# One product of 512 columns for both parts of x in the feature-major projections of a two-layer decoder kernel

## The chip, the cores and the metric

The kernel runs on one core of a Trainium2 chip. The metric is the time of one execution on the device in microseconds, as a median of runs. Within the core TensorE multiplies matrices into accumulators in PSUM, VectorE and ScalarE do elementwise work, GpSimd does a little, and SyncE issues the loads and stores. The profile calls them PE, DVE, ACT, POOL and SP; PEld is TensorE's loading of weights.

## The reference

Two layers run over 256 tokens of 2048 features in float32. Each layer normalises its input, projects it to eight branches of 1024 features (the second layer has 16 columns more), lets two mixers work on the branches, gates their results, projects back and adds. The projections are nearly all of the arithmetic:

```python
def even_layer(h, w_in, w_out, ...):
    proj = jnp.einsum('bld,de->ble', h, w_in).astype(f32)
    hq, hf, hi, hz, dq, dk, dv, dz = jnp.split(proj, 8, axis=-1)
    o_a = hgrn2_recurrence(silu(hq), k_in, log_f, hi)      # k_in, log_f from hf
    o_b = diff_attention(dq, dk, dv, lam_vec, lam_init)
    mixed = concatenate([rmsnorm(o_a) * silu(hz), rmsnorm(o_b) * (1 - lam_init) * silu(dz)])
    return jnp.einsum('ble,ed->bld', mixed, w_out)

def odd_layer(h, w_in, w_out, conv_w, ...):
    proj = jnp.einsum('bld,de->ble', h, w_in).astype(f32)
    cq, ck, cv, cz, ca, cb, sq, sk, sv, sz = jnp.split(proj, splits, axis=-1)
    q, k, v = from silu(causal_conv([cq, ck, cv], conv_w))
    o_c = gated_delta_rule(q, k, v, beta, g)               # beta, g from cb, ca
    o_d = stick_breaking(sq, sk, sv)
    mixed = concatenate([rmsnorm(o_c) * silu(cz), o_d * silu(sz)])
    return jnp.einsum('ble,ed->bld', mixed, w_out)

for layer in range(2):
    x = x + rmsnorm(layer_fn(rmsnorm(x, norm_pre[layer]), ...), norm_post[layer])
```

## The kernel before

**Three products for one.** TensorE multiplies in a float32 format of fewer bits, so each operand is split into a high and a low part, x = xh + xl and w = wh + wl, and a product is wh xh + wh xl + wl xh. The input of a layer lies in SBUF feature-major, 16 blocks of 128 features by 256 tokens, as two pairs of tiles (`act_pair`): the high parts of eight blocks in one tile, the low parts in another.

**Sections.** A branch of 1024 outputs is a section. Token sections (hi, hz, dv, dz; cz, sv) and the output projections (o0, o1) keep x in place as TensorE's weights and send 512 columns of w (346 and 348 in cz); they are in `proj_tok`, L227. Feature sections put w's columns on the partitions, keep w as TensorE's weights and send x's 256 tokens: hf, hq, dq, dk in the first layer and ck, sq, cq, cv, sk, sz in the second, in that order. `feat_section` goes over the 8 heads of such a section; for each, `proj_feat` takes an accumulator bank and two panels of w, [128 rows, 8 blocks, 128 columns], and `mm_feat` sends 8 blocks of each panel: for every block wh with xh and wh with xl, then for every block wl with xh. That makes 24 products a panel and 48 a head, all of 256 columns, all at L261. A result fills half of its bank. The first six heads of hf (`lead`) go together at the start, while x still arrives.

**Panels.** `load_w` issues a panel's load on SyncE's queue into one of 3 buffers, ScalarE casts it to the high part (L212), VectorE subtracts that for the low part (L214); high and low parts have 5 buffers each. So TensorE's work on a panel waits for ScalarE and VectorE, and these wait for TensorE to leave a buffer.

**The way out.** A head's accumulator is multiplied by the rows' 1/rms (`rrow`) by VectorE on the way to SBUF: L377 (`copy_r`) for most sections, L859 in the sections with a convolution (ck, cq, cv), an operation with a further constant in sq. There are 4 banks for projections (`bank_p`) and 4 for the rest (`bank`).

**What sets the order.** A scheduler orders each engine's instructions by priority. Priorities follow the program's text, counted in instructions; panels' loads and splits go 500 ahead of their place (`AHEAD`), the way out of PSUM 500 ahead (`EVAC`), TensorE's work on the mixers 200 and more behind (`LAG` and others), and the forward substitution of the delta rule, long work on VectorE (`gd_inverse`), 600 behind (`FSLAG`). A change in the number of instructions therefore moves these against the panels. Every engine takes its instructions strictly in the order that results. The forward substitution follows section ck; its last steps are the transposes into `xm`.

Of the kernel before, what the change touches and what calls it, by code (L numbers as in the profile page):

```python
# [28 lines left out]
# buffers: [P, 1024] of sections and of mixers, [P, 512], panels as loaded, their high and low parts  # L29
SEC, MIX, TMP, RAW, SPL = 10, 7, 5, 3, 5  # L30
# heads of the first section that start together, products that warm TensorE up
LEAD, WARM = 4, 11
# how many instructions ahead of their place panels' loads and splits and results' way out of PSUM go,
AHEAD, EVAC, SQP = 500, 500, 600
# and how many behind it TensorE's work on the mixers and the forward substitution go
# [3 lines left out]
# Each weight matrix comes as panels [128 rows, nk row blocks, ncol columns], each panel in one piece:  # L39
# (first column, panel's columns, its row blocks) in the panels' order  # L40
# [21 lines left out]
# columns of the packed small parameters  # L62
# [11 lines left out]
def trunk(ctx, tc, x_in, xt_in, small_in, post_in, w_in0, w_out0, w_in1, w_out1, cf_in, cm_in, cx_in, out):  # L74
# [38 lines left out]
    def view(v, offset, *dims):  # L113
        """[step, size] along the row from v's start."""
        return bass.AP(v.tensor, v.offset + offset, [list(v.ap[0])] + [list(d) for d in dims])
# [5 lines left out]
    def load_x(src, name):  # L121
        """x as [tile][half] pieces of 1024 features."""
        xs = [[half(f"{name}{tt}{c}") for c in range(2)] for tt in range(NT)]
        for tt in range(NT):
            for c in range(2):
                nc.sync.dma_start(xs[tt][c], src[tt * P : (tt + 1) * P, c * 1024 : (c + 1) * 1024])
        return xs
# [16 lines left out]
    def at_start(dst, src):  # L144
        """Loads that follow one another."""
        nonlocal before
        with tc.high_priority(), tc.issue_after(before) if before is not None else nullcontext():
            before = ins_of(nc.sync.dma_start(dst, src))
# [24 lines left out]
    strict, later = negm, pair  # the second layer's, in the same place  # L173
# [10 lines left out]
    # TensorE reaches its full clock while the first loads are under way  # L184
# [16 lines left out]
    split_w = [None]  # L201

    def load_w(w, k0, nk, c0, ncol, name, lead=0, behind=None):
        """lead: a panel that meets the start of a layer comes in turn (1), and its low part is made
        on GpSimd (2); behind: an instruction of ScalarE that goes before the panel's."""
# [11 lines left out]
    def proj_tok(act, w, c0, ncol, evac, name, late=False, lead=False, behind=None):  # L217
        """late: the second half of the contraction for tile 0 first, so that its rows end early;
        lead: the first half for tile 0 first, as its rows are there early."""
# [34 lines left out]
    def mm_feat(ps, act, k0, nk, wh, wl):  # L254
        """The low part of w comes last: it is ready last."""
        for part in ((0, 1), (2,)):
            for k in range(nk):
                xh, xl = act(k0 + k)
                for i in part:
                    a, b = ((wh, xh), (wh, xl), (wl, xh))[i]  # L260
                    nc.tensor.matmul(  # L261
                        ps, a[:, k, :], b, start=(k0 + k == 0 and i == 0), stop=(k0 + k == KT - 1 and i == 2)
                    )

    def proj_feat(act, w, c0, evac, name):
        ps = bank_p(f"pf{name}")[:, :T]
# [5 lines left out]
    def act_pair(name):  # L272
        hi = wp.tile([P, 8, T], F32R, tag="acth", bufs=3, name=f"{name}h")
        lo = wp.tile([P, 8, T], F32R, tag="actl", bufs=3, name=f"{name}l")
        return hi, lo
# [9 lines left out]
    def split_rows(pair, j, src, gain, name):  # L285
        """Two blocks of 128 features, src(tt, j), turned feature-major, scaled by gain, split."""
        hi, lo = pair
# [15 lines left out]
    def other_table(func, vs, before=None):  # L303
        """In place: a function of another table set, with Ln's and Exp's loaded again behind it."""
# [6 lines left out]
    def rsqrt_small(o, ssq, scale, eps=None):  # L311
        """o = 1 / sqrt(v), v = ssq * scale + eps: p = c / sqrt(v) from Ln and Exp, then the Newton
        step (3 c^2 - v p^2) p with 2 c^3 = 1. Returns Exp's instruction."""
# [21 lines left out]
    def act_of(pairs):  # L335
        return lambda k: (pairs[k // 8][0][:, k % 8, :], pairs[k // 8][1][:, k % 8, :])

    def row_rstd(xs, tt, o, junk):
        """o [P, 1]: the reciprocal root mean square of tile tt's rows."""
# [6 lines left out]
    # A layer's input goes into the products without its rows' 1/rms, which they take up afterwards:  # L346
    # rs [t, tile] on the token rows, rrow [every partition, t] on the feature rows.
    def split_cols(layer, pairs, xs, d, tt):
        """512 features of a tile turned feature-major, scaled by the gain, split."""
        hi, lo = pairs[d // 2]  # L350
# [13 lines left out]
    def norm_rows(layer, rs, mm=mm):  # L364
        """rs [t, tile] as the rows of rrow."""
# [10 lines left out]
        def copy_r(h, ps, d):  # L376
            nc.vector.tensor_tensor(d, ps, rrow, ALU.mult)  # L377
# [3 lines left out]
    def head_rms(ps, osb, rms, name, eps=None):  # L381
        """ps: four heads of 128 in PSUM -> osb in SBUF, rms [P, 4] of each head."""
# [7 lines left out]
    def gated_mix(o, rms, z, gain, name):  # L390
        """o, z: halves [tt, 4 heads * 128]; rms [P, (tt, head)]."""
# [16 lines left out]
    def out_proj(layer, pairs, w, xsrc, after):  # L408
        """x + rmsnorm(mixed @ w) in place of x; after(tt, d, xs) follows each 512 new columns of a tile."""
# [46 lines left out]
    def feat_section(act, w, c0, name, evac, after=None, lead=None):  # L456
        """A section as two halves [4 heads, 256 tokens] with the features on the partitions.
        lead: the first heads' accumulators, where they have been filled before."""
# [19 lines left out]
    # ======================= layer 0 =======================  # L478
# [3 lines left out]
    def split_xt(k):  # L482
        (hi, lo), v, g = pairs0[k // 8], xT[k // 4][:, k % 4 * T : (k % 4 + 1) * T], pre_gain(0, k)
# [10 lines left out]
    def square_sums(behind):  # L494
        """The rows' sums of squares over the partitions, after the sums over the feature blocks."""
# [18 lines left out]
    # The first heads of the first section go through the first half of the contraction together,  # L514
    # while the rest of the input arrives.
    lead = [(bank_p if i < LEAD else bank)(f"pfhf{i}")[:, :T] for i in range(LEAD + 2)]
# [28 lines left out]
    # lower bounds: softmax over the one even layer, minus itself  # L545
# [9 lines left out]
    # minus lambda of the differential attention  # L555
# [28 lines left out]
    # HGRN2: every pair (s, t) meets at one level, where s is left and t right of a block's middle.  # L584
    # k takes up the decay from s to the middle and q that from there to t, both products of gates
    # that grow from level to level; no factor is above one. The first level takes s = t with it: on
    # the right k is divided by the gate that q takes up there, which is no smaller than FLOOR.
    # A further level needs left rows and right columns only, so that two tiles share its products:
    # tile 1's k on the left and tile 0's q on the right against tile 0's k and tile 1's q. Tile 1's
    # scores, [s, t], fill the upper triangle and tile 0's, [t, s], the lower one, till they are turned.  # L590
# [3 lines left out]
    def hg_scores(hb, q4):  # L594
# [20 lines left out]
        # For level m, from 1024 * g on: k of tile g and q of tile 1 - g of the four heads, in turn the  # L615
# [605 lines left out]
```

## Time and profile before

| | before |
|---|---|
| median of 3 runs | 1049.72 us |
| lowest and highest run | 1047.94 and 1051.91 us |
| profiled execution, first to last instruction | 1049.5 us |
| TensorE busy | 1033.0 us in 6829 products |
| VectorE busy | 688.6 us in 1134 instructions |
| ScalarE busy | 581.7 us in 959 instructions |

The profiled execution is one run; its span is 0.2 us below the median. An engine's busy time counts when it works, not whether anything waits for it. The chain that ended last is followed backwards from the last instruction, at each step to what released it. Products on TensorE overlap, so that a product's own duration is longer than the distance to the next one; a count over a stretch without waits gives the distance. Columns of rows are named with their groups below.

### The profile page before, as it was taken

What the parts mean: (1) busy time and instruction counts of PE and PEld (TensorE: products, weight loads), DVE (VectorE), ACT (ScalarE), POOL (GpSimd) and SP (SyncE); (2) the same over time, 40 slices, a digit from 0 to 9 for tenths busy, and PEclk for the clock granted to TensorE, in tenths of its full rate; (3) what the DMA queues carried; (4) which work ended last, traced back from release to release, by engine and by line L of the source; (5) the groups of instructions that cost most, each with busy time, mean ns of one, the idle gap of its engine ahead of it and who ended that gap; (6) DMA issues with size and microseconds to landing.
All of it is one profiled execution on the core that took longest, in us unless ns stands there. A gap on an engine that the chain in (4) does not pass through costs nothing.

```text
span 1049.5 us, 17359 instructions
## 1 busy us (share of the span) xinstructions
PE 1033.0 (98%) x6829; PEld 943.6 (90%) x6829; DVE 688.6 (66%) x1134; ACT 581.7 (55%) x959; POOL 24.1 (2%) x26
## 2 busy tenths in 40 slices
PE   8999999999999999999899999999999999999996
PEld 7999888899997788888799999999999988998885
DVE  6787976585465655654665866999852855565554
ACT  6656654473355555544476687346565546455441
POOL 0000000000000000000300010000000001000000
PEclk9999999999999999999899999999999999999999
DMA  8665455546545456766376655545750354576652
GB/s 280 200 215 180 138 167 154 188 144 180 183 157 159 148 180 183 263 196 182 114 210 222 190 187 194 165 149 179 215 182 22 101 179 143 164 228 192 199 190 91
DMA packets 53968, 183.98 MB, mean 175 GB/s; under 512 B 6256, under 2 KB 6528, under 8 KB 53888
## 3 DMA queue, kind: packets, MB, share of 16 engines
q1 hardware_dynamic: 53888, 182.89, 54.9%
q8 instruction: 53, 0.87, 0.3%
q14 instruction: 27, 0.22, 0.1%
HBM read 178.66 MB, written 4.20 MB: 174 GB/s over the span
## 4 chain that ended last, share of the span: by engine, by line
PE 96%; DVE 1%; issue 1%; ACT 1%; DMA 1%; POOL 0%; SPq 0%; DVEq 0%; ACTq 0%; POOLq 0%
PE pto L227 16%; PE pfdk L261 4%; PE pfhf L261 4%; PE pfck L261 4%; PE pfcq L261 4%; PE pfcv L261 4%; PE pfdq L261 4%; PE pfsq L261 4%; PE pfhq L261 4%; PE pfsk L261 4%; PE ptdv L227 4%; PE pthi L227 4%; PE ptdz L227 4%; PE pthz L227 4%; PE ptcz L227 4%; PE pfsz L261 4%
## 5 line engine op out<-in xcount | busy, mean ns | idle before, releaser
L214 DVE TENSOR_TENSOR lo<-ro,ho 128x1024 fp32r<-128x1024 f32 x64 | 78.2, 1225 | 68.4 <-ACT ho L212 68.2
L212 ACT CAST ho<-ro 128x1024 fp32r<-128x1024 f32 x64 | 67.4, 1055 | 83.4 <-PE pto L227 63.0
L212 ACT CAST hdk<-rdk 128x1024 fp32r<-128x1024 f32 x16 | 16.8, 1047 | 29.3 <-PE pfdk L261 20.2
L214 DVE TENSOR_TENSOR ldz<-rdz,hdz 128x1024 fp32r<-128x1024 f32 x16 | 19.6, 1225 | 19.6 <-ACT hdz L212 19.6
L214 DVE TENSOR_TENSOR lhz<-rhz,hhz 128x1024 fp32r<-128x1024 f32 x16 | 19.6, 1225 | 18.1 <-ACT hhz L212 18.1
L214 DVE TENSOR_TENSOR ldv<-rdv,hdv 128x1024 fp32r<-128x1024 f32 x16 | 19.6, 1224 | 15.8 <-ACT hdv L212 15.2
L212 ACT CAST hsv<-rsv 128x1024 fp32r<-128x1024 f32 x16 | 16.8, 1052 | 21.2 <-PE ptsv L227 14.5
L212 ACT CAST hdv<-rdv 128x1024 fp32r<-128x1024 f32 x16 | 16.8, 1052 | 21.2 <-PE ptdv L227 13.9
L214 DVE TENSOR_TENSOR lsv<-rsv,hsv 128x1024 fp32r<-128x1024 f32 x16 | 19.6, 1223 | 13.3 <-ACT hsv L212 13.3
L212 ACT CAST hhz<-rhz 128x1024 fp32r<-128x1024 f32 x16 | 16.9, 1055 | 20.3 <-PE pthz L227 18.3
L214 DVE TENSOR_TENSOR lsk<-rsk,hsk 128x1024 fp32r<-128x1024 f32 x16 | 19.5, 1222 | 11.8 <-ACT hsk L212 9.6
L214 DVE TENSOR_TENSOR lsz<-rsz,hsz 128x1024 fp32r<-128x1024 f32 x16 | 19.5, 1222 | 11.6 <-ACT hsz L212 11.4
L214 DVE TENSOR_TENSOR ldk<-rdk,hdk 128x1024 fp32r<-128x1024 f32 x16 | 19.5, 1221 | 11.5 <-ACT hdk L212 11.5
L214 DVE TENSOR_TENSOR lsq<-rsq,hsq 128x1024 fp32r<-128x1024 f32 x16 | 20.0, 1253 | 10.8 <-ACT hsq L212 10.7
L212 ACT CAST hhi<-rhi 128x1024 fp32r<-128x1024 f32 x16 | 16.9, 1054 | 17.3 <-PE pthi L227 11.0
L212 ACT CAST hdz<-rdz 128x1024 fp32r<-128x1024 f32 x16 | 16.8, 1053 | 17.3 <-PE ptdz L227 13.7
L212 ACT CAST hdq<-rdq 128x1024 fp32r<-128x1024 f32 x16 | 16.7, 1048 | 17.2 <-PE pfdq L261 11.3
L227 PE MATMUL pto<-lo,mxbh 128*128 128x512 f32 x64 | 26.2, 409 | 0.0
L212 ACT CAST hsk<-rsk 128x1024 fp32r<-128x1024 f32 x16 | 16.8, 1048 | 16.7 <-PE pfsk L261 9.2
L227 PE MATMUL pto<-ho,mxbl 128*128 128x512 f32 x64 | 25.8, 403 | 0.0
L214 DVE TENSOR_TENSOR ldq<-rdq,hdq 128x1024 fp32r<-128x1024 f32 x16 | 19.6, 1223 | 9.3 <-ACT hdq L212 9.2
L214 DVE TENSOR_TENSOR lck<-rck,hck 128x1024 fp32r<-128x1024 f32 x16 | 19.6, 1223 | 9.3 <-ACT hck L212 9.1
(542 smaller groups left out, 3768.9 us busy)
## 6 DMA issues: line engine op xcount, KB each, us to landing
ro<-in_w_out SPq DMA_DIRECT2D x64, 512.0 KB, 3.8
rhq<-in_w_in SPq DMA_DIRECT2D x16, 512.0 KB, 4.3
rhi<-in_w_in SPq DMA_DIRECT2D x16, 512.0 KB, 3.6
rhz<-in_w_in SPq DMA_DIRECT2D x16, 512.0 KB, 3.6
rdq<-in_w_in SPq DMA_DIRECT2D x16, 512.0 KB, 3.6
rdk<-in_w_in SPq DMA_DIRECT2D x16, 512.0 KB, 3.6
rdv<-in_w_in SPq DMA_DIRECT2D x16, 512.0 KB, 3.6
rdz<-in_w_in SPq DMA_DIRECT2D x16, 512.0 KB, 3.7
```

Of the source, the lines that this page charges most:

```text
L212: split_w[0] = ins_of(nc.scalar.copy(wh, raw))
L214: (nc.gpsimd if lead == 2 else nc.vector).tensor_tensor(wl, raw, wh.bitcast(F32), ALU.subtract)
L227: nc.tensor.matmul(ps[tt][:, :ncol], a[:, cs(tt)], b[:, k, :], start=(k0 + k == 0 and i == 0), stop=(k0 + k == KT - 1 and i == 2),)
L261: nc.tensor.matmul(ps, a[:, k, :], b, start=(k0 + k == 0 and i == 0), stop=(k0 + k == KT - 1 and i == 2))
```

## The change

In feature sections the high and low part of a block of x lie side by side in one tile, [128, 8 blocks, 2, 256], so that one product of 512 columns sends both against wh. Its result fills the whole bank: the first half has wh xh, the second wh xl. The products of wl with xh go to the first half as before. On the way out `joined` copies the second half to SBUF on ScalarE and adds it to the first on VectorE, and the factor of the rows is multiplied in place behind that. A head then has 16 products of 512 columns and 16 of 256. The token sections read the same parts through views of the joint tile and keep their products. The scratch memory of the DMA queues is also given as 4096 bytes at the end of the file. The core of the difference:

```diff
     def mm_feat(ps, act, k0, nk, wh, wl):
-        for part in ((0, 1), (2,)):
-            for k in range(nk):
-                xh, xl = act(k0 + k)
-                for i in part:
-                    a, b = ((wh, xh), (wh, xl), (wl, xh))[i]
-                    nc.tensor.matmul(
-                        ps, a[:, k, :], b, start=(k0 + k == 0 and i == 0), stop=(k0 + k == KT - 1 and i == 2)
-                    )
+        for k in range(nk):
+            nc.tensor.matmul(ps, wh[:, k, :], act(k0 + k, both=True), start=k0 + k == 0, stop=False)
+        for k in range(nk):
+            nc.tensor.matmul(ps[:, :T], wl[:, k, :], act(k0 + k)[0], start=False, stop=k0 + k == KT - 1)
+
+    def joined(ps, d):
+        v = tp.tile([P, T], F32, tag="jn", bufs=2, name=f"jn{next(serial)}")
+        nc.scalar.copy(v, ps[:, T:])
+        nc.vector.tensor_tensor(d, ps[:, :T], v, ALU.add)
 
     def proj_feat(act, w, c0, evac, name):
-        ps = bank_p(f"pf{name}")[:, :T]
+        ps = bank_p(f"pf{name}")
...
     def act_pair(name):
-        hi = wp.tile([P, 8, T], F32R, tag="acth", bufs=3, name=f"{name}h")
-        lo = wp.tile([P, 8, T], F32R, tag="actl", bufs=3, name=f"{name}l")
-        return hi, lo
+        v = wp.tile([P, 8, 2, T], F32R, tag="act", bufs=3, name=name)
+        return v[:, :, 0, :], v[:, :, 1, :], v.rearrange("p k a t -> p k (a t)")
...
     def act_of(pairs):
-        return lambda k: (pairs[k // 8][0][:, k % 8, :], pairs[k // 8][1][:, k % 8, :])
+        def parts(k, both=False):
+            v = pairs[k // 8]
+            return v[2][:, k % 8, :] if both else (v[0][:, k % 8, :], v[1][:, k % 8, :])
+
+        return parts
...
         def copy_r(h, ps, d):
-            nc.vector.tensor_tensor(d, ps, rrow, ALU.mult)
+            joined(ps, d)
+            nc.vector.tensor_tensor(d, d, rrow, ALU.mult)
...
-    lead = [(bank_p if i < LEAD else bank)(f"pfhf{i}")[:, :T] for i in range(LEAD + 2)]
+    lead = [(bank_p if i < LEAD else bank)(f"pfhf{i}") for i in range(LEAD + 2)]
...
             v = tp.tile([P, T], F32, tag="cvt", bufs=2, name=f"cv{name}{h}")
-            nc.vector.tensor_tensor(v, ps, rrow, ALU.mult)
+            joined(ps, v)
+            nc.vector.tensor_tensor(v, v, rrow, ALU.mult)
...
-    sqf = feat_section(
-        act, wi, so, "sq",
-        lambda h, ps, d: nc.vector.scalar_tensor_tensor(d, ps, sbs, rrow, op0=ALU.mult, op1=ALU.mult),
-    )
+    def copy_scaled(h, ps, d):
+        joined(ps, d)
+        nc.vector.scalar_tensor_tensor(d, d, sbs, rrow, op0=ALU.mult, op1=ALU.mult)
+
+    sqf = feat_section(act, wi, so, "sq", copy_scaled)
...
-    nc = bacc.Bacc("TRN2", target_bir_lowering=False, num_devices=1)
+    nc = bacc.Bacc("TRN2", target_bir_lowering=False, num_devices=1, dynamic_dma_scratch_size=4096)
```

How the instructions stand changes at three places that matter. On TensorE, at the end of section dk's first head, where `hT0` is x, `hdk` and `ldk` are the high and low part of a panel, and `h` and `l` behind `hT0_1` are x's parts, before:

```order
L261 MATMUL pfdk0_2738<-hT0_1h_126,hdk0_8_2771 128x256
L261 MATMUL pfdk0_2738<-hT0_1l_127,hdk0_8_2771 128x256
L261 MATMUL pfdk0_2738<-hT0_1h_126,ldk0_8_2773 128x256 x8
L261 MATMUL pfdk1_2800<-hT0_0h_124,hdk1_0_2803 128x256
L261 MATMUL pfdk1_2800<-hT0_0l_125,hdk1_0_2803 128x256
```

and after, the whole of that head and the start of the next:

```order
L258 MATMUL pfdk0_2423<-hT0_0_124,hdk0_0_2426 128x512 x8
L260 MATMUL pfdk0_2423<-hT0_0_124,ldk0_0_2428 128x256 x8
L258 MATMUL pfdk0_2423<-hT0_1_125,hdk0_8_2448 128x512 x8
L260 MATMUL pfdk0_2423<-hT0_1_125,ldk0_8_2450 128x256 x8
L258 MATMUL pfdk1_2472<-hT0_0_124,hdk1_0_2475 128x512 x8
```

The alternating pairs of 256 have become runs of eight of 512; the eight of the low part follow as before. On ScalarE, in section dq around the casts of panels 5 to 7 (`hdq2_8` is the second panel of head 2, `rs` and `sqa` belong to the mixer of hf and hq), before:

```order
L301 ACT_TABLE_LOAD
L212 CAST hdq2_8_2396<-rdq2_8_2394 128x1024
L212 CAST hdq3_0_2428<-rdq3_0_2426 128x1024
L318 ACTIVATE rs3_1854<-ssa01_1852,kc_119 128x4
L385 ACTIVATE sqa11_1871<-oa1_1_1861 128x512
L323 ACTIVATE rs3_1854<-rs3_1854,kc_119 128x4
L212 CAST hdq3_8_2458<-rdq3_8_2456 128x1024
```

and after:

```order
L304 ACT_TABLE_LOAD
L212 CAST hdq2_8_2151<-rdq2_8_2149 128x1024
L212 CAST hdq3_0_2178<-rdq3_0_2176 128x1024
L265 COPY jn21_2073<-pfdq0_2028 128x256
L321 ACTIVATE rs19_1644<-ssa01_1642,kc_119 128x4
L393 ACTIVATE sqa11_1661<-oa1_1_1651 128x512
L326 ACTIVATE rs19_1644<-rs19_1644,kc_119 128x4
L212 CAST hdq3_8_2200<-rdq3_8_2198 128x1024
```

The copy of head 0's second half stands between the casts of panels 6 and 7. On VectorE, around the end of the forward substitution (the transposes into `xm`) in sections cq and cv (`lcv2_0` is the low part of a panel of cv, the operations on `cq1` and `cv1` are steps of the convolution), before:

```order
L969 TENSOR_REDUCE xb_6221<-pr_6222 128x16
L972 STREAM_TRANSPOSE xm_5500<-xb_6221 32x16x16x2 x2
L859 TENSOR_TENSOR cvcq7_7361<-pfcq7_7300,rrow1_5009 128x256
L214 TENSOR_TENSOR lcv2_0_7543<-rcv2_0_7539,hcv2_0_7541 128x1024
L862 SCALAR_TENSOR_TENSOR cq1_6795<-cvcq7_7361,sm_76,cq1_6795 128x255
```

and after:

```order
L868 TENSOR_TENSOR cvcv4_6931<-cvcv4_6931,rrow1_4587 128x256
L214 TENSOR_TENSOR lcv7_0_7053<-rcv7_0_7049,hcv7_0_7051 128x1024
L871 SCALAR_TENSOR_TENSOR cv1_6669<-cvcv4_6931,sm_76,cv1_6669 128x255
L981 STREAM_TRANSPOSE xm_5078<-xb_5695 32x16x16x2
L871 SCALAR_TENSOR_TENSOR cv1_6669<-cvcv4_6931,sm_76,cv1_6669 128x254
L214 TENSOR_TENSOR lcv7_8_7075<-rcv7_8_7071,hcv7_8_7073 128x1024
L871 SCALAR_TENSOR_TENSOR cv1_6669<-cvcv4_6931,sm_76,cv1_6669 128x253
L981 STREAM_TRANSPOSE xm_5078<-xb_5695 32x16x16x2
L214 TENSOR_TENSOR lsk0_0_7513<-rsk0_0_7509,hsk0_0_7511 128x1024
```

The end of the substitution has moved from cv's third head back to the last panel of cv, just ahead of sk's first low part.

## Rows read from the trace of the kernel before

**Rows 1.** The page's busy time, share of the span and instructions of each engine.

```profile
PE 1033.0 (98%) x6829; PEld 943.6 (90%) x6829; DVE 688.6 (66%) x1134; ACT 581.7 (55%) x959; POOL 24.1 (2%) x26
```

**Rows 2.** The page's chain that ended last, share of the span by engine.

```profile
PE 96%; DVE 1%; issue 1%; ACT 1%; DMA 1%; POOL 0%; SPq 0%; DVEq 0%; ACTq 0%; POOLq 0%
```

**Rows 3.** What TensorE waited for: us in total, times, longest us; the whole list.

```profile
PE trh L355 <- issue: 1.4, 1, 1.4
PE trh L355 <- DVE xr L435: 1.3, 1, 1.3
PE idle L189 <- DVE kc L197: 1.2, 1, 1.2
PE ptcz L227 <- POOL lcz L214: 1.2, 1, 1.2
PE sa L279 <- DVE sbr L1103: 0.9, 2, 0.7
PE pfhf L261 <- ACT hT_0h L484: 0.8, 1, 0.8
PE pfhf L261 <- ACT hlead L526: 0.6, 2, 0.4
```

**Rows 4.** The chain in order of time: start us, us, engine, tile, line, instructions.

```profile
166.78 36.08 PE pthz L227 x159
...
262.46 38.40 PE pfdk L261 x320
...
761.90 23.04 PE pfsk L261 x192
...
953.83 87.08 PE pto L227 x384
```

**Rows 5.** Groups by line and shape: count, busy us, mean ns, idle before and releasers.

```profile
L212 ACT CAST hdk<-rdk 128x1024 fp32r<-128x1024 f32 x16 | 16.8, 1047 | 29.3 <-PE pfdk L261 20.2 <-PE pfdq L261 9.1
...
L928 DVE SCALAR_TENSOR_TENSOR nl<-kk,gd,dlo 128x128 f32<-128x128 f32 x16 | 4.6, 345 | 1.3 <-ACT dlo L920 1.3
...
L377 DVE TENSOR_TENSOR dk<-pfdk,rrow 128x256 f32<-128x256 f32 x8 | 3.4, 425 | 10.3 <-PE pfdk L261 10.3
...
L754 ACT COPY wt<-dt 128x256 f32<-128x256 f32 x8 | 3.1, 386 | 0.0
...
L664 DVE TENSOR_TENSOR kq<-kq,tot 128x256 f32<-128x256 f32 x2 | 0.8, 416 | 0.1
```

**Rows 6.** VectorE's timeline, hf's first results: start us, us, line, operation, count.

```profile
43.80 1.42 DVE L377 TENSOR_TENSOR hf<-pfhf,rrow 128x256 f32<-128x256 f32 x4
```

**Rows 7.** Timeline, low parts of cq and sk and their first use, same columns.

```profile
655.08 1.22 DVE L214 TENSOR_TENSOR lcq<-rcq,hcq 128x1024 fp32r<-128x1024 f32 x1
...
666.21 1.12 PE L261 MATMUL pfcq<-hT_0h,lcq 128*128 128x256 f32 x8
...
703.15 1.22 DVE L214 TENSOR_TENSOR lcq<-rcq,hcq 128x1024 fp32r<-128x1024 f32 x1
...
706.53 1.12 PE L261 MATMUL pfcq<-hT_0h,lcq 128*128 128x256 f32 x8
...
750.76 1.22 DVE L214 TENSOR_TENSOR lsk<-rsk,hsk 128x1024 fp32r<-128x1024 f32 x1
...
763.66 1.12 PE L261 MATMUL pfsk<-hT_0h,lsk 128*128 128x256 f32 x8
```

**Rows 8.** Busy time by stretch; columns in the first row.

```profile
core 0: us, PE busy (x) PEld busy (x) DVE busy (x) ACT busy (x) POOL busy (x), PEclk, DMA share, GB/s
653.45:751.98 98.53, 98.53 (x827) 98.53 (x826) 92.98 (x166) 50.49 (x84) 0.00 (x0) 1.00 0.55 173
653.45:704.37 50.92, 50.92 (x427) 50.92 (x425) 49.30 (x99) 22.16 (x24) 0.00 (x0) 1.00 0.48 156
620.00:665.00 45.00, 45.00 (x379) 45.00 (x378) 32.58 (x63) 33.45 (x74) 5.72 (x4) 1.00 0.57 186
60.00:110.00 50.00, 50.00 (x416) 49.73 (x416) 40.45 (x68) 31.68 (x43) 1.31 (x1) 1.00 0.60 189
```

More of the change, by code (lines that the diff above doesn't have):

```diff
@@ L285, in split_rows @@
     def split_rows(pair, j, src, gain, name):
-        hi, lo = pair
+        hi, lo = pair[:2]
         ps = bank(f"tr{name}_{j}")
@@ L348, in split_cols @@
     def split_cols(layer, pairs, xs, d, tt):
-        hi, lo = pairs[d // 2]
+        hi, lo = pairs[d // 2][:2]
         ps = bank(f"trh{layer}_{d}{tt}")
@@ L482, in split_xt @@
     def split_xt(k):
-        (hi, lo), v, g = pairs0[k // 8], xT[k // 4][:, k % 4 * T : (k % 4 + 1) * T], pre_gain(0, k)
+        (hi, lo, _), v, g = pairs0[k // 8], xT[k // 4][:, k % 4 * T : (k % 4 + 1) * T], pre_gain(0, k)
         nc.scalar.activation(hi[:, k % 8, :], v, AF.Copy, scale=g)
@@ L1132, in gate_d @@
         nc.vector.tensor_tensor(z, z, od[hb], ALU.mult)
-        hi, lo = (v[:, hb * 4 : hb * 4 + 4, :] for v in mix_d)
+        hi, lo = (v[:, hb * 4 : hb * 4 + 4, :] for v in mix_d[:2])
         nc.scalar.copy(hi, r4(z))
```

## The prediction

> **What bounds the kernel now.** The page's busy line comes first: TensorE is busy for 1033.0 of 1049.5 us, VectorE for 688.6, ScalarE for 581.7 [rows 1]. A busy engine need not be the one that sets the time, so the chain of work that ended last is read next: 96% of it is TensorE [rows 2]. The list of what TensorE waited for is the check on both. It has seven entries and the largest is 1.4 us [rows 3]. So TensorE works through its own list nearly from end to end, and anything that shortens that list shortens the run, as long as the operands of the shorter list still come in time.
>
> How long is one product? A single duration cannot tell, since products overlap; the spacing can. In the chain by time [rows 4] a stretch of pfdk takes 38.40 us for 320 products of 256 columns, 120.0 ns each, and pfsk's 23.04 us for 192 are 120.0 ns too. The token sections and the output projection send 512 columns: pto takes 87.08 us for 384, 226.8 ns each, and pthz 36.08 us for 159, 226.9 ns. Doubling the columns adds 106.8 ns, so 256 columns alone are worth 106.8 ns and a product has about 13.2 ns that do not depend on its width. Each of these products, narrow or wide, has its own weight load, so that part is met once per product whatever its width.
>
> **The change part by part: TensorE.** For each block of 128 features, a feature section now sends w's high part twice, once against x's high part and once against its low part. After the change it is sent once, against both. Two products of 120.0 ns (240.0) become one of 226.8, and 13.2 ns go. There are 10 feature sections with 8 heads of 16 blocks: 1280 pairs, so 1280 x 13.2 ns = **16.9 us**. The bounds come from reading the spacings to 0.1 ns: 12.8 to 13.5 ns, or 16.4 to 17.3 us. All of it lies on TensorE's list. The third product, w's low part against x's high part, stays as it is.
>
> **The way out.** A head's result now stands in two halves of its bank. Per head ScalarE copies one half to SBUF and VectorE adds the other; the multiplication by the rows' factor that VectorE did before then reads SBUF. That is 80 copies and 80 additions more. The nearest rows are a ScalarE copy out of PSUM of the same size, 386 ns, and VectorE's multiplication out of PSUM, 425 ns; four of these in a row take 1.42 us, 355 ns each [rows 5, 6]. So ScalarE gets 80 x 0.386 = 31 us more work, VectorE 80 x 0.355 to 0.425 = 28 to 34 us. The moved multiplication is taken at its old price, as one from SBUF to SBUF took 416 ns [rows 5]. Beside TensorE this costs nothing where those engines have room: with the additions VectorE has 717 to 723 us of work against about 1030.
>
> A head also leaves its bank about 0.8 us later (copy 0.386, addition 0.425). The feature sections have four banks of their own, so the bank is next wanted three heads later; one head is 48 products now, 5.76 us, and after it 16 x (226.8 + 120.0) ns = 5.55 us. The cover is some 16 us. Without it the 0.8 us would be paid per head.
>
> **ScalarE's order.** ScalarE also casts the panels whose low parts VectorE then makes, and it takes its instructions in the order that they stand in. The order shows the copy for a head behind the cast of the sixth panel after that head's first, so the next cast waits for that head's products, and the addition in VectorE's order waits with it. What is queued behind is the cast of panel 7 of the section, while TensorE has panels 2 to 6 still to do: five half heads of 2.77 us, 13.9 us. Copy, cast and low part take 0.386 + 1.047 + 1.22 = 2.7 us [rows 5, 7]. The old cast also waited for TensorE there (of 29.3 us idle before pfdk's casts, 20.2 were for pfdk's own products) [rows 5], since it wants that head's buffer. I put nothing on it in the middle of the run.
>
> **VectorE where it has no room.** The stretch from sq's last low part to sk's first, 653.45 to 751.98 us, is the one to look at: 92.98 us of VectorE's work in 98.53 [rows 8]. Others have room: 32.58 in 45.00 and 40.45 in 50.00. The time by which a low part is ready before TensorE wants it tells how near VectorE is. For cq's first panel it is ready at 656.30 and wanted at 666.21, a lead of 9.9 us; for cq's fifteenth 704.37 against 706.53, 2.2 us, the shortest of these sections; for sk's first 751.98 against 763.66, 11.7 us [rows 7].
>
> If only the 2.2 counted, cq would stall: by then VectorE has some 7 additions more (2.5 to 3.0 us), and eight of the nl products (0.345 us each, 2.8) [rows 5], which the order now places behind sq's low parts, while TensorE comes 14 x 0.106 = 1.5 us sooner. That is 6.8 to 7.3 against 2.2, a stall of about 5. But the order also moves the forward substitution back: its last transposes stood beside cv's fifth low part, and now stand just before sk's first. So I reckon over the whole stretch. VectorE's work becomes 92.98 + 16 additions (5.7 to 6.8) + 2.8 = 101.4 to 102.6 us; TensorE's way from cq's first low part to sk's first was 97.45 us and loses 32 x 0.106 = 3.4. Of that, 2.85 us lie before cq's first low part is ready, so VectorE has 98.6 to 99.8 us left against TensorE's 94.1: it loses 5 to 6 us of a lead of 9.9 and need not stop TensorE. The lead at the beginning can be smaller than now, since ck's second half of mixing work also stands later; I allow up to 4 us less, an estimate from the work that passes. The stall lies between 0 and 4 us; I take **1.5**, nearer to zero because the whole stretch still balances.
>
> **The start, and small waits.** TensorE already waits there for the first x and the first panel (0.8 and 0.6 us) [rows 3]. The first wide product wants x's low part too, and copies now stand among the first casts: 0 to 1 us, taken as 0.5. The products of the mixers stand later among the panels by the count of instructions. Their waits now sum to a few us over the run, none above 1.4 [rows 3]; a new position can cost or save 2 us, taken as zero. The end of the run, from the last product of pto to the stores, is not touched.
>
> **The sum.** The profiled execution's span is 1049.5 us, 0.2 below the median of 1049.72. From the median: 1049.7 - 16.9 + 1.5 + 0.5 = 1034.8, so **1035 us**. Bounds of the terms: 1049.7 - 17.3 - 2 = 1030.4 and 1049.7 - 16.4 + 4 + 1 + 2 = 1040.3.
>
> **Rivals.** *VectorE paces cq.* The stall of 5 us computed for cq alone comes in full, and with the smaller lead at the beginning up to 4 more: 1032.8 + 0.5 + 5 to 9 is 1038 to 1042; two us more by other waits, 1044. For it: 49.30 us of work in cq's 50.92 [rows 8] and the 2.2 us. Against it: the substitution's move, and that the stretch as a whole balances.
>
> *The wide product saves nothing.* The 13.2 ns might belong to a switch of the accumulated operand and be paid for each 256 columns; then a wide product takes the pair's 240.0 and the time is 1049.7 + 0 to 2. Against it stands the spacing of 226.8 with 512 columns in the same number format, on the same engine [rows 4]. The Trainium skill, page "TensorE: Matmul & The Clock Gate", section "Back-to-back issue gap", gives an isolated product N/2.4 + 2.5 ns, by which joining two saves only 2.5 ns, 3.2 us in all (an estimate from that page); the trace does not agree, with 13.2 ns beside its 2.5.
>
> *Slower: VectorE's additions show in full.* VectorE makes the low parts that TensorE cannot go on without, at 32 panels per two sections. If it paced TensorE through the feature sections, each addition of up to 0.42 us would be added to the time: 34 - 16.9 = 17 us more, 1067. It becomes slower than before from the point where more than half of the additions (40 of 80) lie open. Against it: outside the one stretch of 98.53 us VectorE has about 596 us of work in 951, and a low part is ready a panel or more ahead.
>
> **How the numbers follow.** About 0.5%, 5.2 us, is what a measurement of this kernel can tell from no change. My forecast, 1030 to 1038, has 0.80; VectorE pacing cq, 1038 to 1044, 0.12; no saving, 1049 to 1052, 0.05; slower 0.03. The first two are faster by over 0.5% (below 1044.5): 0.92. Nothing saved is within it: 0.05. Slower: 0.03. The range runs over the bounds of the terms, 1030.4 to 1041, and leaves out the upper part of the cq case and the other two.
>
> **What would show it.** Right, step by step: 5549 products on TensorE in place of 6829; in a stretch of panels alone one of 512 and one of 256 columns together take 346.8 ns, a head 5.55 us; VectorE some 717 to 723 us busy and ScalarE about 613; TensorE's chain about 16 us shorter. The middle sections (dq, dk, ck) should each be 1.7 us shorter. The weak step shows between 640 and 740 us: waits of TensorE for a low part of cq or cv by VectorE; over 4 us of these and the cq case holds. Wrong would be a spacing of wide products near 240 ns, or waits for low parts in dq, dk or ck, where VectorE has room.

## The result and the profile after

| | before | after |
|---|---|---|
| median of 4 runs each | 1049.93 us | 1035.24 us |
| lowest and highest | 1047.94 and 1051.91 us | 1033.88 and 1037.36 us |
| ratio of the two | | 0.986, 95% interval 0.9846 to 0.9874 |
| profiled execution, first to last instruction | 1049.5 us | 1035.3 us |
| products on TensorE | 6829 | 5549 |

The gain is 14.7 us; the sum of the forecast has 14.9. The page's busy line and its chain by engine, answering [rows 1, 2]:

```profile
PE 1016.3 (98%) x5549; PEld 871.9 (84%) x5549; DVE 714.1 (69%) x1214; ACT 604.3 (58%) x1039; POOL 24.4 (2%) x26
...
PE 88%; DVE 3%; ACT 3%; DMA 3%; issue 2%; SPq 0%; POOL 0%; DVEq 0%; ACTq 0%; POOLq 0%
```

1280 products are gone. VectorE has 714.1 us of work in place of 688.6, ScalarE 604.3 in place of 581.7, and TensorE still is the engine that works nearly from end to end. The chain shows less of it than the 96% of before, because this chain, followed backwards, turns off to panel loads and their casts in some places (DMA and ACT 3% each). Whether TensorE stood still for them, the list of waits tells. The whole of it, answering [rows 3] (us in total, times, longest us):

```profile
PE pfhf L258 <- DVE hT L493: 1.9, 3, 0.8
PE gc L282 <- DVE gct L844: 1.5, 1, 1.5
PE trh L362 <- issue: 1.4, 1, 1.4
PE trh L362 <- DVE xr L443: 1.3, 1, 1.3
PE idle L189 <- DVE kc L197: 1.2, 1, 1.2
PE ptcz L227 <- POOL lcz L214: 1.2, 1, 1.2
PE pfhf L258 <- ACT hlead L534: 0.7, 1, 0.7
PE pfhf L258 <- ACT hhf L212: 0.5, 1, 0.5
PE dt L286 <- DVE wtok L753: 0.4, 1, 0.4
```

None waits for a low part of cq or cv, which was the weak step. New are `gc`, a small product of the delta rule, and the wait for x's low part (`hT`) at the start.

What does a panel cost now? TensorE's timeline in section dk (start us, us, line, operation, operands, count), answering [rows 4]:

```profile
271.84 2.00 PE L258 MATMUL pfdk<-hT,hdk 128*128 128x512 f32 x8
273.68 1.12 PE L260 MATMUL pfdk<-hT,ldk 128*128 128x256 f32 x8
274.64 2.00 PE L258 MATMUL pfdk<-hT,hdk 128*128 128x512 f32 x8
276.48 1.11 PE L260 MATMUL pfdk<-hT,ldk 128*128 128x256 f32 x8
277.43 2.00 PE L258 MATMUL pfdk<-hT,hdk 128*128 128x512 f32 x8
```

Read the starts, not the durations, since products overlap. Eight wide products take 273.68 - 271.84 = 1.84 us, 230 ns each, and eight narrow ones 274.64 - 273.68 = 0.96, 120 ns each. A panel comes round every 2.79 us (2.793 over longer stretches), where 8 x (226.8 + 120.0) ns had been expected, 2.774. So a wide product costs about 229.1 ns here, not the 226.8 of the token sections. The single starts show where it goes: behind a run of narrow products the first five wide ones stand 233, 236, 228, 233 and 231 ns apart, the next 227; at the other end the first narrow one is 7 ns short. Some 20 ns a panel remain.

The way out, by line and form (count, busy us, mean ns, idle before), answering [rows 5]:

```profile
L266 DVE TENSOR_TENSOR dk<-pfdk,jn 128x256 f32<-128x256 f32 x8 | 3.3, 418 | 0.0
...
L385 DVE TENSOR_TENSOR dk<-dk,rrow 128x256 f32<-128x256 f32 x8 | 3.4, 424 | 0.2
...
L265 ACT COPY jn<-pfdk 128x256 f32<-128x256 f32 x8 | 3.0, 372 | 0.0
```

Addition 418 ns, moved multiplication 424, copy 372, all near the prices that were taken. Busy time rose by less than these durations add up to: 80 additions have 33.5 us and VectorE 25.5 us more, 80 copies 29.5 us and ScalarE 22.6 more. The durations of neighbours on one engine overlap, as TensorE's do, and busy time counts a moment once. The stretch that was to be tight, by the clock times of before and then from sq's last low part to sk's first as they lie now, answering [rows 8] (columns as there); then the low part of cq's last panel and the first of sk, each with its first use, answering [rows 7]:

```profile
653.00:752.00 99.00, 99.00 (x588) 87.62 (x588) 97.28 (x186) 56.27 (x101) 0.00 (x0) 1.00 0.54 168
643.21:745.45 102.24, 102.24 (x609) 90.50 (x608) 98.75 (x189) 61.16 (x116) 2.85 (x2) 1.00 0.56 174
```

```profile
693.32 1.22 DVE L214 TENSOR_TENSOR lcq<-rcq,hcq 128x1024 fp32r<-128x1024 f32 x1
...
700.53 1.12 PE L260 MATMUL pfcq<-hT,lcq 128*128 128x256 f32 x8
...
744.22 1.23 DVE L214 TENSOR_TENSOR lsk<-rsk,hsk 128x1024 fp32r<-128x1024 f32 x1
...
753.35 1.12 PE L260 MATMUL pfsk<-hT,lsk 128*128 128x256 f32 x8
```

VectorE is busy for 97.28 of 99 us, and yet TensorE never stops: all 99 us are busy, and so are all 102.24 of the second stretch. The low part is ready at 694.54 and wanted at 700.53, 6.0 us ahead, and that is the shortest lead in cq. The first of sk is ready at 745.45, 7.9 us ahead.

### The profile page after: what moved, and what is told of

It reads as the page before. It is cut to its first block, busy times and chain, and to the rows that moved or that the text cites. A ratio compares the mean times of both kernels' runs of the same rounds, so it can differ in the third digit from the quotient of the medians.

```text
span 1035.3 us, 14993 instructions
## 1 busy us (share of the span) xinstructions
PE 1016.3 (98%) x5549; PEld 871.9 (84%) x5549; DVE 714.1 (69%) x1214; ACT 604.3 (58%) x1039; POOL 24.4 (2%) x26
## 4 chain that ended last, share of the span: by engine, by line
PE 88%; DVE 3%; ACT 3%; DMA 3%; issue 2%; SPq 0%; POOL 0%; DVEq 0%; ACTq 0%; POOLq 0%
PE pto L227 16%; PE ptdv L227 4%; PE pthz L227 4%; PE ptdz L227 4%; PE ptsv L227 4%; PE pthi L227 4%; PE pfsq L258 3%; PE pfdq L258 3%; PE pfcv L258 3%; PE pfcq L258 3%; PE pfdk L258 3%; PE pfhq L258 3%; PE pfsk L258 3%; PE pfsz L258 2%; PE pfhf L258 2%
## 5 line engine op out<-in xcount | busy, mean ns | idle before, releaser
L227 PE MATMUL ptcz<-hcz,hT 128*128 128x346 f32 (+1 forms) x192 | 46.6, 325 | 0.0
L227 PE MATMUL ptdv<-hdv,hT 128*128 128x512 f32 x128 | 42.6, 403 | 0.0
L227 PE MATMUL pthi<-hhi,hT 128*128 128x512 f32 x128 | 42.0, 401 | 0.0
L227 PE MATMUL pto<-ho,mxb 128*128 128x512 f32 x128 | 40.6, 396 | 0.0
L227 PE MATMUL ptsv<-hsv,hT 128*128 128x512 f32 x128 | 40.1, 393 | 0.0
L227 PE MATMUL ptdz<-hdz,hT 128*128 128x512 f32 x128 | 40.1, 393 | 0.0
L227 PE MATMUL pto<-ho,mxa 128*128 128x512 f32 x128 | 39.9, 391 | 0.0
L227 PE MATMUL pthz<-hhz,hT 128*128 128x512 f32 x128 | 39.8, 392 | 0.0
L227 PE MATMUL pto<-ho,mxc 128*128 128x512 f32 x128 | 39.5, 389 | 0.0
L227 PE MATMUL pto<-ho,mxd 128*128 128x512 f32 x128 | 39.4, 389 | 0.0
L258 PE MATMUL pfsq<-hT,hsq 128*128 128x512 f32 x128 | 33.5, 397 | 0.0
```

Of the source, the lines that this page charges most:

```text
L227: nc.tensor.matmul(ps[tt][:, :ncol], a[:, cs(tt)], b[:, k, :], start=(k0 + k == 0 and i == 0), stop=(k0 + k == KT - 1 and i == 2),)
L258: nc.tensor.matmul(ps, wh[:, k, :], act(k0 + k, both=True), start=k0 + k == 0, stop=False)
```

## The experiments

Each was compared with the kernel before on the same chip; its median there is given where it matters.

**The way out alone.** The products are as narrow as before, but the second goes to the other half of the bank and copy and addition stay.

```diff
-            nc.tensor.matmul(ps, wh[:, k, :], act(k0 + k, both=True), start=k0 + k == 0, stop=False)
+            xh, xl = act(k0 + k)
+            nc.tensor.matmul(ps[:, :T], wh[:, k, :], xh, start=k0 + k == 0, stop=False)
+            nc.tensor.matmul(ps[:, T:], wh[:, k, :], xl, start=False, stop=False)
```

> The changed way out alone: w's high part goes through x's high and x's low part in two products of 256 columns again, the second into the bank's other half, and copy and addition stay. If all of the gain lies in the wide product and the way out is hidden, TensorE's list is that of the kernel before and the time is 1049.9 us, with up to 2 us either way by the order. If instead the wide product gave the whole 16.9 us and the way out took 2.2 us of it back, this kernel takes about 1052. If the additions lay open, 28 to 34 us more, about 1080.

Measured: 1050.89 us against 1050.05, ratio 1.0011 (0.9993 to 1.0028). The page's busy line shows that the work was really there:

```profile
PE 1030.3 (98%) x6829; PEld 941.8 (90%) x6829; DVE 717.1 (68%) x1214; ACT 602.4 (57%) x1039; POOL 23.0 (2%) x26
```

VectorE has its 717.1 us, TensorE its 6829 products, and the time is that of before. The interval, -0.7 to +2.9 us, does not exclude a cost of 2 us, but it excludes that any large part of the 28 to 34 us lies open. The other reading in the expectation, 16.9 us from the wide product and 2.2 taken back by the way out, does not fit the panel of 2.793 us above, which gives 13.9. This kernel also keeps the joint tile of x and the 4096 bytes of the DMA queues, so neither of these is the gain: it comes from the wide product. One wait shows how near VectorE is here:

```profile
PE pfcv L262 <- DVE lcv L214: 0.4, 1, 0.4
```

That is a low part of cv, in the order that this kernel's count of instructions gives. With the same way out the changed kernel's order leaves cv some 6 us of lead.

**The way out left away.** The wide product stays and the second half (wh xl) is left out of the result.

```diff
-            joined(ps, d)
-            nc.vector.tensor_tensor(d, d, rrow, ALU.mult)
+            nc.vector.tensor_tensor(d, ps[:, :T], rrow, ALU.mult)
```

> The wide product stays, and its second half (wh xl) is left out of the result: no copy and no addition. If the way out is hidden, the time is that of the changed kernel but for the wait at gc, which can be shorter by up to 1.5 us and the low clock behind it by 2: 1032 to 1035. If the 28 to 34 us of additions lay open to any part, it would be shorter by that part: a tenth of them is 3 us more, 1029 to 1032.

Measured: 1034.74 us (1032.07 to 1039.16), ratio 0.986 (0.9832 to 0.9887); the changed kernel took 1034.13 on the same chip.

```profile
PE 1016.6 (98%) x5549; PEld 872.9 (84%) x5549; DVE 686.5 (66%) x1134; ACT 582.1 (56%) x959; POOL 24.5 (2%) x26
```

VectorE has 27.6 us less work than in the changed kernel (686.5 against 714.1) and ScalarE 22.2 less, and nothing is gained. From both sides, then: adding the way out to the old products costs nothing that can be measured, and taking it from the new ones gives nothing.

**How far the cover goes.** Three more additions per head into a scratch tile that nothing reads.

```diff
         nc.vector.tensor_tensor(d, ps[:, :T], v, ALU.add)
+        for _ in range(3):
+            x = tp.tile([P, T], F32, tag="jx", bufs=2, name=f"jx{next(serial)}")
+            nc.vector.tensor_tensor(x, ps[:, :T], v, ALU.add)
```

> Three more additions of the same halves per head into a scratch tile: 240 more, some 85 to 100 us of VectorE, with nothing that reads them. VectorE then has about 805 of 1035 us, but in the stretch from sq's last low part to sk's first, where it is busy for 97.28 of 99 us now, 48 more additions (17 to 20 us) have no room. If only that stretch lacks cover, TensorE waits there, or for the substitution behind it, for 10 to 20 us: 1045 to 1055. If additions lie open everywhere, 85 to 100 us: above 1115. If VectorE has cover even there, 1035.

Measured: 1057.26 us (1055.97 to 1059.19), ratio 1.0072 (1.0053 to 1.009): 23 us more than the changed kernel's 1034.13 on that chip, for 72.5 us more of VectorE:

```profile
PE 1022.8 (97%) x5549; PEld 876.5 (83%) x5549; DVE 786.6 (75%) x1454; ACT 603.4 (57%) x1039; POOL 25.7 (2%) x26
```

The 240 additions were expected at 85 to 100 us; their durations do add up to 100, and busy time rises by 72.5. About a third of that shows, in few places. TensorE's waits, the four longest (us in total, times, longest us), then the busy time in the stretch that was to lack cover and in one behind each of the four waits (columns as in [rows 8]):

```profile
PE gc L285 <- DVE gd L835: 4.0, 1, 4.0
PE pfsk L258 <- DVE jx L269: 3.9, 1, 3.9
PE pfhf L260 <- DVE lhf L214: 3.5, 1, 3.5
PE xt L289 <- DVE xm L984: 2.4, 1, 2.4
```

```profile
653.00:760.00 107.00, 107.00 (x639) 94.78 (x638) 102.92 (x214) 68.02 (x136) 2.59 (x2) 1.00 0.60 183
37.00:43.00 6.00, 5.75 (x22) 5.27 (x23) 5.66 (x14) 1.67 (x3) 0.00 (x0) 0.50 0.73 238
627.50:630.00 2.50, 2.50 (x14) 2.50 (x13) 1.47 (x3) 2.50 (x10) 0.00 (x0) 0.50 0.45 174
791.50:794.00 2.50, 2.50 (x9) 2.02 (x8) 2.50 (x9) 1.10 (x4) 0.00 (x0) 0.50 0.17 66
818.50:821.00 2.50, 2.50 (x14) 2.50 (x13) 2.50 (x6) 1.76 (x3) 0.00 (x0) 0.50 0.02 7
```

The first stretch is the surprise. From 653 to 760 us TensorE is busy for all 107.00 us, although VectorE is busy for 102.92 of them. The low parts stand ahead of the mixers' work in VectorE's order (the shortest lead of one of cq or cv is 5.3 us), so what is pushed back is that work: the small product gc waits for `gd` (4.0 us, near 622 us), the substitution's result `xm` is late for xt (2.4 us, near 815), and sk waits for a bank that an addition still reads (`jx`, 3.9 us, near 786). At the start, where panels and x arrive together, a low part itself is late (3.5 us, near 33). The four waits sum to 13.8 us, and behind each the granted clock is 0.50: 13.5 us in the windows shown, of which half is lost, 6.7 us (an estimate from the clock). Together that is 20.5 of the 23 us. The additions also count as instructions and so move the mixers' work among the panels; how much of the waits comes from VectorE's load and how much from the moved order, this run does not separate. The place came true only for the wait behind the substitution, 2.4 us, the size, 1045 to 1055, was somewhat too small, and the mechanism "VectorE paces the low parts" was seen at the start alone.

**A wait that came with the order.** In the changed kernel's first profile the second group of gc waits 1.46 us for a VectorE copy that reads the first group's result in the same bank. Windows around and behind it (columns as in [rows 8]):

```profile
582.00:585.00 3.00, 1.54 (x9) 1.14 (x8) 2.49 (x7) 2.03 (x4) 0.00 (x0) 0.94 0.64 199
585.00:588.00 3.00, 3.00 (x11) 2.71 (x12) 1.67 (x5) 0.37 (x3) 0.00 (x0) 0.50 0.55 168
588.00:595.00 7.00, 7.00 (x41) 6.10 (x41) 3.10 (x6) 5.66 (x6) 0.00 (x0) 1.00 0.50 150
```

The granted clock is 0.94 around the wait and then 0.50, the lower of the engine's two levels (1.2 and 2.4 GHz), until 588 us: the stretch from 580 to 600 us is 3.7 us longer than its products' spacings. The experiment gives the second group a bank of its own.

```diff
+    ps = bank("gcs")
     mm(ps[:, 0:16], upper, g8.rearrange("p a h -> p (a h)"), start=True, stop=True)
```

> The second group of the small products called gc gets a bank of its own, so that it needn't wait for the copy that reads the first group's. In the changed kernel TensorE waits there for 1.46 us at 582.7 us, and then runs at a granted clock of 0.50 up to 588 us; the stretch from 580 to 600 us has 3.7 us beyond its products' spacings, against 0.5 in the kernel before. If the wait brings the lower clock with it, both go: 3.2 us, 1032.0. If the clock's fall has another reason, only the wait goes: 1033.7. If the wait only moves to the next of these small products, 1035.2.

Measured: 1035.05 us (1034.29 to 1036.56), ratio 0.9856 (0.9834 to 0.9879). In its trace wait and low clock are gone:

```profile
582.00:585.00 3.00, 3.00 (x19) 2.70 (x19) 2.97 (x8) 1.99 (x5) 0.00 (x0) 1.00 0.65 197
585.00:588.00 3.00, 3.00 (x18) 2.63 (x17) 2.93 (x5) 1.98 (x2) 0.00 (x0) 1.00 0.75 235
```

The span of that one execution is 1032.5 us, 2.8 below the changed kernel's profiled one. But the medians, from different chips, were 0.2 us apart, so both kernels were run once more on one chip.

> The changed kernel again, beside the others of this call on one chip: 1035 us, a ratio of 0.986, with the wait at the second group of gc and the lower clock behind it in its trace again.

> The kernel with a bank of its own for the second group of gc, on the same chip as the changed kernel. In its first trace the wait and the lower clock are gone (0.4 us beyond the spacings from 580 to 600 us in place of 3.7) and the span is 1032.5. If that is what the kernel gains, its median stands 3 us below the changed kernel's, a ratio of 0.997. If the wait is one of many that come and go from run to run, the two medians agree within 1 us.

Measured: 1034.13 us for the changed kernel (ratio 0.9854, 0.9834 to 0.9873), 1034.4 with the own bank (0.9852, 0.9832 to 0.9871). No difference. The changed kernel's own trace says why; its wait for gc, and the same stretches:

```profile
PE gc L282 <- DVE gct L844: 0.9, 1, 0.9
```

```profile
575.00:582.00 7.00, 6.05 (x34) 4.59 (x33) 6.52 (x13) 4.25 (x6) 0.00 (x0) 1.00 0.72 224
582.00:585.00 3.00, 3.00 (x20) 2.67 (x20) 2.40 (x6) 0.68 (x4) 0.00 (x0) 1.00 0.47 168
585.00:588.00 3.00, 3.00 (x20) 2.67 (x20) 1.75 (x3) 2.97 (x3) 0.00 (x0) 1.00 0.55 175
```

This time the wait was 0.9 us and the clock stayed at 1.00; the span was 1031.8. The 3.7 us were what one execution happened to lose, and that execution was the slowest of its four (1037.36 us). A wait at this place exists, 0.6 to 1.5 us in three profiles, but its removal is worth less than the runs can tell.

**How the runs of wide and narrow products matter.** First longer runs: 16 wide products for a head's two panels, then 16 narrow ones.

```diff
-        for k0 in range(0, KT, 8):
-            mm_feat(ps, act, k0, 8, *load_w(w, k0, 8, c0, P, f"{name}_{k0}"))
+        held = [(k0, *load_w(w, k0, 8, c0, P, f"{name}_{k0}")) for k0 in range(0, KT, 8)]
+        for k0, wh, wl in held:
+            for k in range(8):
+                nc.tensor.matmul(ps, wh[:, k, :], act(k0 + k, both=True), start=k0 + k == 0, stop=False)
+        for k0, wh, wl in held:
+            for k in range(8):
+                nc.tensor.matmul(ps[:, :T], wl[:, k, :], act(k0 + k)[0], start=False, stop=k0 + k == KT - 1)
```

> The wide products of both panels of a head come first, 16 in a row, then the 16 narrow ones. If the 20 ns are paid once per run, 74 runs fewer save 1.5 us: a head takes 5.57 us in place of 5.587, and the time is 1033.7. If they belong to the wide product as such, a head stays at 5.587 and the time at 1035.2.

Measured: 1039.42 us (1036.99 to 1040.96), ratio 0.9894 (0.9868 to 0.992), where the kernel with the own bank for gc had 1035.05 on the same chip. Yet the products did what was expected of runs. TensorE's timeline in dk:

```profile
270.70 3.82 PE L273 MATMUL pfdk<-hT,hdk 128*128 128x512 f32 x16
274.35 2.08 PE L276 MATMUL pfdk<-hT,ldk 128*128 128x256 f32 x16
276.27 3.82 PE L273 MATMUL pfdk<-hT,hdk 128*128 128x512 f32 x16
```

A head comes round every 276.27 - 270.70 = 5.57 us, in place of 5.587, which fits 20 ns paid once per run; from its first to its last product dk takes 44.41 us in place of 44.57. What was lost lies elsewhere, in part in waits of the mixers (us in total, times, longest us):

```profile
PE gc L287 <- DVE gct L849: 2.1, 1, 2.1
PE xt L291 <- ACT bv L1045: 1.8, 1, 1.8
```

With both edits, long runs and the own bank, on one chip with the changed kernel:

> The changed kernel for the third time, beside a kernel that joins two edits: 1034 to 1035 us. Products of feature sections as in its first two traces (dk from its first to its last product 44.57 us); what differs between its traces is a wait at gc of 0.9 to 1.5 us and stretches at the lower clock.

> Both edits: the wide products of a head's two panels in one run of 16, and a bank of its own for the second group of gc. The runs save 1.3 to 1.5 us of products for certain (dk 44.41 us in place of 44.57); the wait at gc, 2.1 us and a stretch at the lower clock in the kernel with the long runs alone, should go. If the time lost there and at xt was only that, the median stands 1 to 2 us below the changed kernel's. If a head that needs both panels before its low parts begin keeps other work waiting, as at xt (1.8 us), it stands level or above.

Measured: 1034.7 us for the changed kernel (ratio 0.9858, 0.9842 to 0.9875), 1036.82 with both edits (0.9879, 0.9861 to 0.9897). The wait at gc is gone, dk again takes 44.41 us, and the wait at xt has become the longest:

```profile
PE xt L291 <- ACT bv L1046: 2.5, 1, 2.5
```

TensorE waits there for ScalarE's work on `bv`. The first section, hf, is longer as well: from its first to its last product 51.3 and 51.2 us in the two kernels with long runs, 48.4 to 50.5 in six profiles of kernels with runs of eight (the changed one, the one with the own bank, the one without the way out). The shorter products did not make up for this; why hf is longer was not tested. The intervals overlap, so "not better" is what is shown.

Then the shortest runs: each narrow product directly behind its wide one.

```diff
         for k in range(8):
             nc.tensor.matmul(ps, wh[:, k, :], act(k0 + k, both=True), start=k0 + k == 0, stop=False)
-        for k in range(8):
             nc.tensor.matmul(ps[:, :T], wl[:, k, :], act(k0 + k)[0], start=False, stop=k0 + k == KT - 1)
```

> Behind every wide product of a block stands at once the narrow one of the low part, so that the runs of eight of each kind are gone (not in the first six heads of hf). In the changed kernel a panel takes 2.793 us, 0.019 more than 8 x 346.8 ns, the excess in the first five wide products behind a run of narrow ones. If each step from a narrow to a wide product costs these 20 ns, 1036 more steps cost 21 us: 1056. If the excess is something that a run of narrow products builds up and wide ones work off, there is none left or as much as now: 2.774 to 2.793 us a panel, 1032 to 1035.

Measured: 1038.41 us (1037.82 to 1039.43), ratio 0.9888 (0.9866 to 0.9909). Neither forecast: 20 ns a step would have given 1056, none at all 1032 to 1035. The trace shows two rhythms in one kernel, in dk and in a later section (start us, us, line, operation):

```profile
269.94 0.40 PE L273 MATMUL pfdk<-hT,hdk 128*128 128x512 f32 x1
270.17 0.28 PE L274 MATMUL pfdk<-hT,ldk 128*128 128x256 f32 x1
...
271.35 0.40 PE L273 MATMUL pfdk<-hT,hdk 128*128 128x512 f32 x1
```

```profile
616.71 0.39 PE L273 MATMUL pfsq<-hT,hsq 128*128 128x512 f32 x1
616.94 0.28 PE L274 MATMUL pfsq<-hT,lsq 128*128 128x256 f32 x1
...
618.10 0.39 PE L273 MATMUL pfsq<-hT,hsq 128*128 128x512 f32 x1
```

In dk four pairs take 271.35 - 269.94 = 1.41 us, and over the section the distances 120 and 236, 113 and 233, 117 and 241 ns repeat, 353.3 ns a pair; in sq four pairs take 618.10 - 616.71 = 1.39, and 117 and 230 ns repeat, the 346.8 that the two kinds cost apart. dk takes 45.11 us from first to last product in place of 44.57. So the excess is not a fixed price of a step from narrow to wide. The distances of dk are also those of hq, dq, cq, cv and sk, those of sq also of ck. The slower rhythm costs dk 45.11 - 44.57 = 0.54 us; six such sections make up the 3.2 us by which this kernel is slower than the changed one. What sets the rhythm stays open.

## Why the prediction was right, and where its steps were off

**The term of the product was too large.** The step "two products of 120.0 ns become one of 226.8" took the wide product's price from the token sections, where only products of 512 follow one another. Between runs of narrow ones it costs 229.1, a panel 2.793 us in place of 2.880. That is 0.087 x 160 panels = 13.9 us, below the bound of 16.4. The Trainium skill's formula for an isolated product (page "TensorE: Matmul & The Clock Gate", section "Back-to-back issue gap"), by which 3.2 us were to be saved (an estimate from that page), does not agree with these 13.9 us.

**The term of VectorE was too large as well.** The stall of 1.5 us (0 to 4) did not come. The reckoning over the whole stretch was the right one. From sq's last low part to sk's first VectorE was to have 101.4 to 102.6 us of work and had 98.75; TensorE's way from cq's first low part to sk's first was to take 94.1 us and took 94.72 (658.63 to 753.35). The recorded numbers, 98.6 to 99.8 against 94.1, give a loss of 4.5 to 5.7 us of lead, not 5 to 6; the lead fell by 4.0, from 11.9 at cq's first panel to 7.9 at sk's.

The allowance for a smaller lead at the beginning, where the stall was taken from, was the wrong step: that lead grew from 9.9 to 11.9 us. In the first profile no lead from cq to sk was under 5.7 us, against the 2.2 of before, in an order that puts the low parts ahead and has the substitution moved back. That the order would decide it was said; how fully was not. The way out alone, in another order, had a wait of 0.4 us for a low part of cv, so the danger was real.

**The two errors went opposite ways,** 3.0 us too much gain and 1.5 us too much stall, and the half microsecond at the start cannot be told from the spread: waits of hf's products sum to 3.1, 1.7 and 1.3 us in three profiles of the changed kernel, 1.4 before. With 13.9 and no stall the same sum gives 1036.3. That forecast and result agree within 0.5 us is luck; that the time lies within the range is not. Over all 33 runs of before and 12 of after that were made here the medians are 1049.92 and 1034.65 us, 15.3 us apart. 13.9 of these are products. The remaining 1.3 us are not located: two profiles of the changed kernel, with the same products, differ by 3.5 us in span (1035.3 and 1031.8).

**The base was read wrongly by 2 us, without effect.** Each run's time stands 1.8 to 2.1 us above the span of the same execution in the runs of both kernels that list it (1037.36 and 1035.3, 1033.87 and 1031.8). The profiled execution of before with its 1049.5 thus was a run of some 1051.4 us, above the median, not 0.2 below it. The sum was made from the median, which kept it right.

**Order.** "A new position can cost or save 2 us" was the term for the mixers' moves. In the first profile the stretch at gc lost 3.2 us more than before. Other places gave some back: from 500 to 520 us the granted clock was 0.91, and 0.83 before. The bound was fair for a median and too narrow for one execution.

**The signs.** 5549 products came. A wide and a narrow product together take 349.1 ns and a head 5.587 us, where 346.8 and 5.55 were named. VectorE's 714.1 us and ScalarE's 604.3 lie below the 717 to 723 and 613, since durations were added that overlap. That dq, dk and ck would each be 1.7 us shorter did not come so: dq is 1.3 shorter (47.77 to 46.45 us from first to last product), dk 7.2 (51.76 to 44.57), because the 30 mixers' products that stood within it have gone elsewhere, and ck 0.0 to 2.5 in three profiles. The sign takes a count of a section's own products, not its length. The range is given twice, to 1038 and to 1041; the result lies in both.

**The rivals.** That VectorE paces cq: no wait of TensorE for a low part there, even with 72.5 us more on VectorE. That the wide product saves nothing: refuted by the panel of 2.793 us. Slower by open additions: refuted from both sides, by the way out alone and by its absence.

## What to carry to other kernels

Where one engine works from end to end, a fixed part per instruction is worth collecting: joining two products that share their weights saved 10.9 ns of each pair, and 80 copies of 0.37 us and 80 additions of 0.42 us on engines with room cost nothing measurable. Take the price of the new form from a stream with the same neighbours, not from a uniform one. And before a stall in one trace is hunted, profile the same kernel again: the one that looked worth 3 us was gone in the next execution.

## What was not expected of the hardware

- Products of 512 columns that alternate with runs of 256 stand further apart than in a stream of their own: 229.1 against 226.8 ns in runs of 8, 227.9 in runs of 16 (from 44.41 us for dk), and in strict alternation the pair takes 353.3 (dk) or 346.8 ns (sq) in different sections of one execution.
- A wait of 1.46 us was followed by 3 us at the lower clock in one execution; one of 2.0 us in the alternating kernel was not (2.5 us lost from 580 to 600 us in all, and a granted clock of 1.00 from 575 to 595 us). All four waits of 2.4 to 4.0 us in the kernel with three more additions were. For the shorter ones the wait's length alone does not decide it here.
